# Attention scores of a two-layer encoder: the products with the low parts of K as pairs of 64-row tiles

## The chip, the cores and the metric

The kernel runs on one core of a Trainium2 chip. The metric is the time of one execution on the device in microseconds (us), the median of three runs. The engines named below are PE (TensorE, which multiplies; PEld are its weight loads), DVE (VectorE), ACT (ScalarE), POOL (GpSimd) and SP (SyncE, which issues most DMAs). A change of 0.2% is about the least that a measurement of this kernel can tell from none.

## What is computed

The reference is a stack of two layers over 256 tokens of 1024 channels. Each layer has one combined input projection, three mixers (a short convolution, a pooling mixer, attention), a gated sum through W_o, and a SwiGLU feed-forward block. What the change touches is the scores of the attention:

```
scores = einsum("bnqhgd,bnkhd->bhgnqk", qb, kb) * HEAD_DIM ** -0.5     # 16 heads, 4 KV heads, HEAD_DIM 64
scores = where(valid, scores + bias, NEG_INF)                         # |key - query| <= 128, T5 bias
m = maximum(max(scores), sink);  p = exp(scores - m)
p = p / (sum(p) + exp(sink - m));  out = einsum(p, v)
```

With 256 tokens and a window of 128 on both sides, each block of 128 queries sees all 256 keys, and the mask rides in the bias.

## The kernel before

All matrix work is done in split precision: an fp32 operand is held as a high part (rounded, type fp32r) and a low part (what is left), and a product is the sum of three products, high by high, high by low and low by high (`mm3`, lines 160 to 164). Weights come as blocks of 128 x 128 in the order in which they are used; `convert` (lines 128 to 137) splits 8 blocks at a time into `hi` (ACT) and `lo` (DVE). The program is 7877 products on PE, and almost all are of one kind: load a 128 x 128 block, stream 256 columns against it.

Attention is done for two heads at a time, in 8 groups `t` per layer, 16 in the program. `qs[t]` holds two tiles of 128 rows, one per head `j` of the group: for head 0 the 64 rows 0 to 63 are the high parts of Q and rows 64 to 127 the low parts; for head 1 it is the other way round. For each KV head, `kk[v][0]` holds the high parts of K twice, in both halves of the rows, so that one product of 128 rows gives high Q by high K plus low Q by high K. `kk[v][1]` holds the low parts of K in the 64 rows that carry the high parts of Q, and zeros in the other 64 (set once, line 206). One product of 128 rows with it gives high Q by low K; half of its rows multiply by zero.

`att_scores` (lines 340 to 365) makes for each of two blocks `b` of 128 queries and each head `j` those two products, 8 in all, into a PSUM bank per block `b`: the halves of the bank are the two heads. DVE then reads each half, adds the bias and takes the row maximum in one instruction (line 353); ACT takes the exponentials (line 358), and DVE multiplies by the reciprocal of the sum (line 363). `att_transpose` transposes the probabilities on PE (line 374), `att_pv` multiplies by V (line 389).

These steps are sprinkled into the long projection: `tick()` is called after each output tile of the projection (24 products of PE), and the table `steps` says that the scores of group `t` go at tick 4 + int(4.3 t), its transposes 4 ticks later and its products with V 6 ticks later (constants SC0, SCD, TRD, PVD on line 768). Where the transposes of one group and the scores of the next fall on one tick, the scores go first. PSUM has two pools of four banks: `newB` for the projections, `newA` for the scores, transposes and V products of attention, used in rotation.

Of the kernel before, what the change touches and what calls it, by code (L numbers as in the profile page):

```python
# [16 lines left out]
P = 128  # L17
D = 1024
T = 256
# [4 lines left out]
EPS = 1e-6  # L24
NEG = -1e30
# [8 lines left out]


def plan_layer(last):
    """Order in which the 128 x 128 weight blocks (matrix, k, n) of a layer are used."""
    out = []

    def inner(mat, ns, nk=KT):  # L40
        for n in ns:
            for k in range(nk):
                out.append((mat, k, n))

    def outer(mat, ns, nk=KT):
        for k in range(nk):
            for n in ns:
                out.append((mat, k, n))

    outer("in", (CK, CK + 1, CV, CV + 1))  # L50
    for q in range(2):
        inner("in", [CQ + 4 * q + j for j in range(4)])
    inner("in", [CGA + n for n in range(8)])
    for n in range(8):
        inner("in", (CC + n, CX + n, CB + n))
    inner("in", (CU, CU + 1))
    inner("a", range(8))
    for n in range(8):
        inner("in", (CGP + n, CGT + n))
        if n % 2 == 1 and n < 7:  # L60
            inner("in", (CU + n + 1, CU + n + 2))
        inner("t", (n,))
        out.extend(("pool", k, n) for k in range(2))
        if n >= 2:
            out.extend(("o", n - 2, m) for m in range(8))
    for j in range(4):
        out.extend(("o", k, m) for k in (6, 7) for m in (2 * j, 2 * j + 1))
    for q in range(NQ):
        ns = (2 * q, 2 * q + 1, FT + 2 * q, FT + 2 * q + 1)
        if q == 0:  # L70
            outer("gu", ns)
        else:
            inner("gu", ns)
        if q >= 1:
            for k in (2 * q - 2, 2 * q - 1):
                out.extend(("down", k, m) for m in range(8))
    ks = (2 * NQ - 2, 2 * NQ - 1)
    if last:
        for k in ks:
            out.extend(("down", k, m) for m in range(8))  # L80
    else:
        for j in range(4):
            out.extend(("down", k, m) for k in ks for m in (2 * j, 2 * j + 1))
    return out
# [6 lines left out]
def trunk(ctx, tc, wst, xT, chp, sinkb, rb, invc, gfin, ident_d, out):  # L91
    nc = tc.nc
    V, S, G, PE = nc.vector, nc.scalar, nc.gpsimd, nc.tensor
# [12 lines left out]
        uid[0] += 1  # L106
        return f"{s}{uid[0]}"

# [1 line left out]
    plan = []  # L110
    for l in range(L):
        plan += [(l,) + key for key in plan_layer(l == L - 1)]
# [55 lines left out]
    def half(j):  # L168
        return slice(j * T, (j + 1) * T)

# [1 line left out]
    warm = const.tile([P, T], F32R, name="warm")  # L172
    V.memset(warm.bitcast(F32), 0.0)
    epst = const.tile([P, 1], F32, name="epst")
# [6 lines left out]
    x = act.tile([P, KT, T], F32, name="x")  # L181
# [9 lines left out]
    V.memset(ones, 1.0)  # L191
    ident = const.tile([P, P], F32, name="ident")
    G.dma_start(ident, ident_d)
    # [0 | I | 0]
    ident2 = const.tile([P, 3 * P], F32R, name="ident2")
    G.memset(ident2.bitcast(F32), 0.0)
    G.tensor_copy(ident2[:, P:2 * P], ident)
# [2 lines left out]
    inv = const.tile([P, 4, 2, 8], F32, name="inv")  # L200
    G.dma_start(inv, invc)

    # kk[kv]: (high parts of K in both halves of the rows, low parts in one half and zeros in the other)
    kk = [[act.tile([P, T], F32R, name=f"kk{v}{i}") for i in range(2)] for v in range(4)]
    for v in range(4):
        V.memset(kk[v][1].bitcast(F32), 0.0)
    ups = [act.tile([P, T + 16], F32, name=f"up{i}") for i in range(2)]
    for u in ups:
        V.memset(u, 0.0)
    # vt[key tile]: per pair of KV heads (a, b) the columns [a high | a low | b low | b high]  # L210
    vt = [act.tile([P, 2, 4, 64], F32R, name=f"vt{kt}") for kt in range(2)]

    stab = dpool.tile([16, 512], F32, name="stab")

    def build_bias():
        """stab[h, i] = rel_bias[bucket(255 - i), h] inside the window, NEG outside."""
        st = tmp.tile([16, 512], F32, name="st", tag="t2", bufs=8)
        G.memset(st, NEG)
        G.tensor_copy(st[:, 248:255], rbt[:, 17:24][:, ::-1])
        G.tensor_copy(st[:, 255:263], rbt[:, 0:8])  # L220
        for i, (a, b) in enumerate(RANGES):
            G.tensor_copy(st[:, 255 - b:256 - a], rbt[:, 24 + i:25 + i].to_broadcast([16, b - a + 1]))
            G.tensor_copy(st[:, 255 + a:256 + b], rbt[:, 8 + i:9 + i].to_broadcast([16, b - a + 1]))
        G.dma_start(stab, st)
# [12 lines left out]
        t = pool.tile([P, 2, T], F32R, name=nm(name), tag=tag, bufs=bufs)  # L237
        return t[:, 0, :], t[:, 1, :]

# [1 line left out]
    def xg_tiles(l, gi, j, st):  # L241
        """x tiles 2j, 2j+1 times the gain, split."""
        for k in (2 * j, 2 * j + 1):
            g = ch[:, l, gi, k:k + 1]
            h, lo = pair(act, "xz", 8, "xg")
            if j < XJ:
                V.tensor_scalar(h, x[:, k], g, None, op0=ALU.mult)  # L247
            else:
                S.activation(h, x[:, k], AF.Copy, scale=g)
            V.scalar_tensor_tensor(lo, x[:, k], g, h.bitcast(F32), op0=ALU.mult, op1=ALU.subtract)  # L250
            st["xg"].append((h, lo))

    def squares(j, st):
        """Squares of x tiles 2j, 2j+1, added up."""
        sq = tmp.tile([P, 2, T], F32, name=nm("sq"), tag="t2", bufs=8)
        S.activation(sq, x[:, 2 * j:2 * j + 2], AF.Square)
        if j == 0:
            st["acc"] = sq
        else:
            G.tensor_tensor(st["acc"], st["acc"], sq, op=ALU.add)  # L260
        if j == 3:
            s1 = tmp.tile([P, T], F32, name=nm("s1"), tag="t1", bufs=10)
            st["add"] = G.tensor_tensor(s1, st["acc"][:, 0], st["acc"][:, 1], op=ALU.add)
            st["sum"] = s1

    def preload(func, src):
        """Has the activation table of func loaded once src is there."""
        d = tmp.tile([P, 1], F32, name=nm("pre"), tag="pre", bufs=2)
        S.activation(d, src, func)

    def rsqrt(r, sd, ms):
        """r = ms ** -0.5 from the table's square root, one Newton step on top."""
        V.reciprocal(r, sd)
        V.tensor_tensor(ms, ms, r, op=ALU.mult)
        V.tensor_tensor(ms, ms, r, op=ALU.mult)
        V.tensor_scalar(ms, ms, -0.5, 1.5, op0=ALU.mult, op1=ALU.add)
        V.tensor_tensor(r, r, ms, op=ALU.mult)
# [13 lines left out]
        st["q"], st["ps"] = rr, ps  # L291

    def norm_rows(st):
        """The tokens' factors as rows, the same on all partitions."""
        rr, ps = st["q"], st["ps"]
        for i in range(4):
            tb = i % 2
            PE.matmul(ps[:, T:], rr[:, i:i + 1].to_broadcast([P, P]), ident2[:, P - tb * P:3 * P - tb * P],
                      start=(i == 0), stop=(i == 3))
        r = tmp.tile([P, T], F32, name=nm("r"), tag="rbc", bufs=2)  # L300
        S.activation(r, ps[:, T:], AF.Copy)
        st["r"] = r
# [21 lines left out]
    def newA(name="a"):  # L324
        return psA.tile([P, 2 * T], F32, name=nm(name), tag="A")
# [10 lines left out]
        for k in range(nk):  # L336
            mm3(dst, (l, mat, k, n), xs[koff + k][0], xs[koff + k][1], start=(k == 0), stop=(k == nk - 1))

# [1 line left out]
    def att_scores(l, t, qs, st):  # L340
        bias = st["bias"].pop(t)
        ss = []
        for b in range(2):
            ps = newA("sc")
            cs = slice(b * P, (b + 1) * P)
            for j in range(2):
                kh, kl = kk[2 * (t // 4) + j]
                PE.matmul(ps[:, half(j)], qs[t][j][:, cs], kh, start=True, stop=False)  # L348
                PE.matmul(ps[:, half(j)], qs[t][j][:, cs], kl, start=False, stop=True)
            s = tmp.tile([P, 2, T], F32, name=nm("s"), tag="t2", bufs=8)  # L350
            sm = tmp.tile([P, 10], F32, name=nm("sm"), tag="sm", bufs=6)
            for j in range(2):
                V.tensor_tensor_reduce(s[:, j], ps[:, half(j)], bias[:, j, b * P:b * P + T], 1.0,
                                       sk[:, l, 2 * t + j:2 * t + j + 1], ALU.add, ALU.max, sm[:, j:j + 1])
            V.tensor_scalar(sm[:, 2:4], sm[:, 0:2], -1.0, None, op0=ALU.mult)  # L355
            V.tensor_tensor(sm[:, 4:6], sk[:, l, 2 * t:2 * t + 2], sm[:, 2:4], op=ALU.add)
# [39 lines left out]
        split(h, lo, f)  # L396
        st["ao"][t] = (h, lo)

# [1 line left out]
    def t1(name):  # L400
        return tmp.tile([P, T], F32, name=nm(name), tag="t1", bufs=10)

    def mixer(l, st):
        xg = st["xg"]
        def kv_out():
            norm_rows(st)
            r = st["r"]
            # K reversed in the tokens
            for p in range(2):
                kf = t1("kf")  # L410
                V.tensor_tensor(kf[:, ::-1], kb[:, half(p)], r, op=ALU.mult)
                for j in range(2):
                    rr = slice(64 * j, 64 * j + 64)
                    other = slice(64 - 64 * j, 128 - 64 * j)
                    kh, kl = kk[2 * p + j]
# [13 lines left out]
        qs = []  # L429
# [73 lines left out]
        def pool_mixer(n, bank, j):  # L503
# [7 lines left out]
            for d in (1, 2, 4)[:g]:  # L511
# [1 line left out]
                lo_, hi_ = lo_ + d, hi_ - d  # L513
                V.tensor_tensor(s2[:, lo_:hi_], s[:, lo_ - d:hi_ - d], s[:, lo_ + d:hi_ + d], op=ALU.add)
                s = s2
            # the ends divide by their own counts: the constant is window / count there
            e = bass.AP(tensor=s.tensor, offset=s.offset + 8, ap=[list(s.ap[0]), [T - 8, 2], [1, 8]])
            V.tensor_tensor(e, e, inv[:, g], op=ALU.mult)
            pf = t1("pf")
# [181 lines left out]
    for l in range(L):  # L701
# [13 lines left out]
        else:  # L715
            fms = [tmp.tile([P, 8], F32, name=nm("fm"), tag="sm", bufs=6) for _ in range(2)]

            def sums(tb):
                """fm[0], fm[1]: sums of squares of the halves; fm[2]: the first as a share of the mean, + EPS."""
                fm = fms[tb]  # L720
                for hh in range(2):
                    y = xn[2 * tb + hh]
# [40 lines left out]
MH = 1  # L763
XJ = 1
POOLW = (2, 4, 8, 16)
# distances in the window that share one of the T5 buckets 8..15 (exact buckets below 8)
RANGES = ((8, 11), (12, 15), (16, 22), (23, 31), (32, 45), (46, 63), (64, 90), (91, 128))
SC0, SCD, TRD, PVD = 4, 4.3, 4, 6

# [63 lines left out]
```

## Time and profile before

| | |
|---|---|
| three runs, us | 981.97, 981.01, 981.03 |
| median, us | 981.03 |
| span of the profiled execution, first to last instruction, us | 980.1 |
| PE busy in it, us (share) | 968.1 (99%) |
| PE weight loads busy, us (share) | 954.4 (97%) |
| DVE busy, us (share) | 715.7 (73%) |
| ACT busy, us (share) | 554.0 (57%) |
| mean granted clock of TensorE, of full speed | 0.998 |

The profile is of one execution; the 0.9 us between its span and the median are what lies outside the first and the last instruction, and how executions differ. Busy times of PE are sums of pieces in which at least one product was running; products overlap, so a single one lasts 0.28 us while the next starts 0.12 us after it.

### The profile page before, as it was taken

How to read it: one execution, taken by the hardware profiler on the slowest of the kernel's cores; microseconds unless marked ns; L12 is line 12 of the kernel's file. 1: busy time of each engine (PE TensorE's matmuls, PEld its weight loads, DVE VectorE, ACT ScalarE, POOL GpSimd, SP SyncE). 2: the span in 40 equal slices, each digit the busy share in tenths (PEclk: the TensorE clock that was granted, in tenths of full speed). 3: DMA queues.
4: the chain of work that ended last, by engine and by line, in shares of the span. 5: the costliest groups of instructions: out<-in, count | busy, mean ns of one | idle time of the engine just before them, and what ended most of it. 6: DMA issues, size and time to landing. Idle time of an engine off the chain costs nothing.

```text
span 980.1 us, 19200 instructions
## 1 busy us (share of the span) xinstructions
PE 968.1 (99%) x7877; PEld 954.4 (97%) x7877; DVE 715.7 (73%) x1332; ACT 554.0 (57%) x931; POOL 45.7 (5%) x66
## 2 busy tenths in 40 slices
PE   8999999999999999999999999999999999999996
PEld 7999999999999999999999999999999999999995
DVE  7899898567668955545589898985777697555554
ACT  5866776654456544444477576765554564444443
POOL 5100000000001000000020000000000020000001
PEclk9999999999999999999999999999999999999999
DMA  8755544555554455455443745445554555545531
GB/s 279 254 193 197 189 161 163 197 180 183 189 199 171 174 189 199 173 178 205 178 172 130 248 163 188 161 143 174 192 193 173 172 194 189 200 170 204 184 129 43
DMA packets 27112, 178.12 MB, mean 182 GB/s; under 512 B 3280, under 2 KB 3808, under 8 KB 6800
## 3 DMA queue, kind: packets, MB, share of 16 engines
q1 hardware_dynamic: 24912, 169.93, 49.1%
q0 software_dynamic: 2112, 6.97, 2.5%
q8 instruction: 61, 1.00, 0.4%
q14 instruction: 27, 0.22, 0.1%
HBM read 175.80 MB, written 1.08 MB: 180 GB/s over the span
## 4 chain that ended last, share of the span: by engine, by line
PE 97%; DMA 1%; DVE 1%; SPq 0%; ACT 0%; issue 0%; DVEq 0%; ACTq 0%
PE b L162 25%; PE b L164 25%; PE b L163 25%; PE dn L164 2%; PE dn L162 2%; PE dn L163 2%; PE dn L617 2%; PE dn L616 2%; PE dn L615 2%; PE wo L162 2%; PE wo L163 2%; PE o L389 2%; PE wo L164 2%; PE pt L374 1%; DMA x<-xT 1%; PE sc L348 1%
## 5 line engine op out<-in xcount | busy, mean ns | idle before, releaser
L136 DVE TENSOR_TENSOR lo<-raw,hi 128x1024 fp32r<-128x1024 f32 (+1 forms) x321 | 390.0, 1222 | 215.2 <-ACT hi L135 214.4
L135 ACT ACTIVATE hi<-raw 128x1024 fp32r<-128x1024 f32 (+1 forms) x321 | 337.2, 1055 | 333.1 <-PE b L163 215.0
L162 PE MATMUL b<-h,hi 128*128 128x256 f32 x1344 | 379.8, 283 | 0.0
L164 PE MATMUL b<-h,lo 128*128 128x256 f32 x1344 | 378.4, 282 | 0.0
L163 PE MATMUL b<-h,hi 128*128 128x256 f32 x1344 | 378.3, 281 | 0.0
L162 PEld LDWEIGHTS b<-h,hi 128*128 128x128 f32 x1344 | 253.2, 188 | 0.2
L163 PEld LDWEIGHTS b<-h,hi 128*128 128x128 f32 x1344 | 253.1, 188 | 0.2
L164 PEld LDWEIGHTS b<-h,lo 128*128 128x128 f32 x1344 | 253.1, 188 | 0.0
L163 PE MATMUL b<-xg,hi 128*128 128x256 f32 x448 | 126.6, 283 | 1.6 <-DVE xg L250 1.6
L162 PE MATMUL b<-xg,hi 128*128 128x256 f32 x448 | 126.3, 283 | 1.1 <-DVE xg L247 0.8
L164 PE MATMUL b<-xg,lo 128*128 128x256 f32 x448 | 126.0, 282 | 0.0
L163 PEld LDWEIGHTS b<-xg,hi 128*128 128x128 f32 x448 | 84.4, 188 | 2.3 <-DVE xg L250 2.2
L162 PEld LDWEIGHTS b<-xg,hi 128*128 128x128 f32 x448 | 84.2, 188 | 1.6 <-issue 1.1
L164 PEld LDWEIGHTS b<-xg,lo 128*128 128x128 f32 x448 | 84.4, 188 | 0.0
L164 PE MATMUL dn<-fa,lo 128*128 128x256 f32 x176 | 49.5, 281 | 0.0
L163 PE MATMUL dn<-fa,hi 128*128 128x256 f32 x176 | 49.5, 281 | 0.0
L162 PE MATMUL dn<-fa,hi 128*128 128x256 f32 x176 | 49.5, 281 | 0.0
L260 POOL TENSOR_TENSOR sq<-sq,sq 128x512 f32<-128x512 f32 x12 | 16.2, 1353 | 507.3 <-DVE xg L250 315.5
L358 ACT ACTIVATE s<-s,sm 128x256 f32<-128x256 f32 x64 | 31.8, 500 | 13.0 <-DVE sm L355 13.0
L162 PE MATMUL b<-z,hi 128*128 128x256 f32 x128 | 36.4, 284 | 0.0
L164 PE MATMUL b<-z,lo 128*128 128x256 f32 x128 | 36.1, 282 | 0.0
L164 PE MATMUL b<-ao,lo 128*128 128x256 f32 x128 | 36.0, 282 | 0.0
(174 smaller groups left out, 1537.9 us busy)
## 6 DMA issues: line engine op xcount, KB each, us to landing
raw<-wst SPq DMA_DIRECT2D x158, 1024.0 KB, 4.9
bias<-stab POOLq DMA_DIRECT2D x16, 384.0 KB, 3.9
raw<-wst SPq DMA_DIRECT2D x3, 512.0 KB, 7.7
out<-xn SPq DMA_DIRECT2D x4, 256.0 KB, 2.0
x<-xT SPq DMA_DIRECT2D x3, 256.0 KB, 8.2
raw<-wst SPq DMA_DIRECT2D x2, 256.0 KB, 4.2
gf<-gfin POOLq DMA_DIRECT2D x2, 256.0 KB, 3.8
x<-xT SPq DMA_DIRECT2D x2, 128.0 KB, 4.6
```

What stands on the lines that cost most here:

```text
L135: S.activation(hi[:, s], raw[:, s], AF.Copy)
L136: V.tensor_tensor(lo[:, s], raw[:, s], hi[:, s].bitcast(F32), op=ALU.subtract)
L162: PE.matmul(dst, wh, xh, start=start, stop=False, skip_group_check=skip)
L163: PE.matmul(dst, wh, xl, start=False, stop=False, skip_group_check=skip)
L164: last_mm[0] = PE.matmul(dst, wl, xh, start=False, stop=stop, skip_group_check=skip)
L260: G.tensor_tensor(st["acc"], st["acc"], sq, op=ALU.add)
L348: PE.matmul(ps[:, half(j)], qs[t][j][:, cs], kh, start=True, stop=False)
L358: S.activation(s[:, j], s[:, j], AF.Exp, bias=sm[:, 2 + j:3 + j], accum_out=sm[:, 6 + j:7 + j])
L389: PE.matmul(ps[:, half(j)], vv, pts[kt][i][:, half(j)], start=(kt == i == 0), stop=(kt == i == 1))
L615: PE.matmul(d, ah[:, cs], wh, start=(k == 0), stop=False)
L616: PE.matmul(d, ah[:, cs], wl, start=False, stop=False)
L617: PE.matmul(d, al[:, cs], wh, start=False, stop=(k == FT - 1))
```

## The change

Only `att_scores` is changed; everything else in the diff are comments that go, and shifted line numbers. The two PSUM banks of a group are now one per head (`banks[j]`), with the two blocks of queries as halves. All four products with the high parts of K come first, as before with 128 rows. Then come the four products with the low parts, each with only those 64 rows that hold something other than zeros: rows 0 to 63 for head 0, rows 64 to 127 for head 1, in turn. A product of 64 rows uses a tile of 64 x 128 of the array; the two heads use the upper and the lower tile. The number of products, the columns that each streams and the sums are the same.

```diff
     def att_scores(l, t, qs, st):
         bias = st["bias"].pop(t)
         ss = []
+
+        banks = [newA("sc") for _ in range(2)]
         for b in range(2):
-            ps = newA("sc")
-            cs = slice(b * P, (b + 1) * P)
             for j in range(2):
-                kh, kl = kk[2 * (t // 4) + j]
-                PE.matmul(ps[:, half(j)], qs[t][j][:, cs], kh, start=True, stop=False)
-                PE.matmul(ps[:, half(j)], qs[t][j][:, cs], kl, start=False, stop=True)
+                PE.matmul(banks[j][:, half(b)], qs[t][j][:, b * P:(b + 1) * P], kk[2 * (t // 4) + j][0],
+                          start=(b == 0), stop=False, skip_group_check=True)
+
+        for b in range(2):
+            for j in range(2):
+                r = slice(64 * j, 64 * j + 64)
+                PE.matmul(banks[j][:, half(b)], qs[t][j][r, b * P:(b + 1) * P], kk[2 * (t // 4) + j][1][r],
+                          start=False, stop=True, skip_group_check=True)
+        for b in range(2):
             s = tmp.tile([P, 2, T], F32, name=nm("s"), tag="t2", bufs=8)
             sm = tmp.tile([P, 10], F32, name=nm("sm"), tag="sm", bufs=6)
             for j in range(2):
-                V.tensor_tensor_reduce(s[:, j], ps[:, half(j)], bias[:, j, b * P:b * P + T], 1.0,
+                V.tensor_tensor_reduce(s[:, j], banks[j][:, half(b)], bias[:, j, b * P:b * P + T], 1.0,
                                        sk[:, l, 2 * t + j:2 * t + j + 1], ALU.add, ALU.max, sm[:, j:j + 1])
```

On PE, the scores of the first group in the program, between two output tiles of the projection (b66). In the rows sc67 and sc70 are the banks of the two blocks of queries; kk00 and kk10 are the high parts of K for the two heads, kk01 and kk11 the low parts. Before:

```order
L164 MATMUL b66_850<-xg8_191,lo16_720 128x256
L348 MATMUL sc67_879<-kk00_133,q31_510 128x256
L349 MATMUL sc67_879<-kk01_134,q31_510 128x256
L348 MATMUL sc67_879<-kk10_135,q31_510 128x256
L349 MATMUL sc67_879<-kk11_136,q31_510 128x256
L348 MATMUL sc70_897<-kk00_133,q31_510 128x256
L349 MATMUL sc70_897<-kk01_134,q31_510 128x256
L348 MATMUL sc70_897<-kk10_135,q31_510 128x256
L349 MATMUL sc70_897<-kk11_136,q31_510 128x256
L162 MATMUL b66_850<-xg1_158,hi17_790 128x256
```

The same place of the changed kernel, where sc67 and sc68 are the banks of the two heads and lines 347 and 353 are the products with the high and the low parts:

```order
L164 MATMUL b66_850<-xg8_191,lo16_720 128x256
L347 MATMUL sc67_879<-kk00_133,q31_510 128x256
L347 MATMUL sc68_880<-kk10_135,q31_510 128x256
L347 MATMUL sc67_879<-kk00_133,q31_510 128x256
L347 MATMUL sc68_880<-kk10_135,q31_510 128x256
L353 MATMUL sc67_879<-kk01_134,q31_510 128x256
L353 MATMUL sc68_880<-kk11_136,q31_510 128x256
L353 MATMUL sc67_879<-kk01_134,q31_510 128x256
L353 MATMUL sc68_880<-kk11_136,q31_510 128x256
L162 MATMUL b66_850<-xg1_158,hi17_790 128x256
```

High and low products no longer alternate: each group has one passage from 128-row products to 64-row tiles and one back, and within the four the tile, the bank and the head alternate.

On DVE, the readers of those banks (ISA stands for the fused add and maximum, and for the read of its accumulator into sm), before:

```order
L353 ISA s68_884,sm69_885<-sc67_879,bias16_342,sk_129 128x256
L353 ISA sm69_885 128x1
L353 ISA s68_884,sm69_885<-sc67_879,bias16_342,sk_129 128x256
L353 ISA sm69_885 128x1
L353 ISA s71_902,sm72_903<-sc70_897,bias16_342,sk_129 128x256
```

and in the changed kernel:

```order
L359 ISA s69_889,sm70_890<-sc67_879,bias16_342,sk_129 128x256
L359 ISA sm70_890 128x1
L359 ISA s69_889,sm70_890<-sc68_880,bias16_342,sk_129 128x256
L359 ISA sm70_890 128x1
L359 ISA s71_902,sm72_903<-sc67_879,bias16_342,sk_129 128x256
```

The readers are the same in number, size and place; they now go from bank to bank, so that both banks are held until the last of the four reads, where the first was free after two.

## Rows read from the trace of the kernel before

**Rows 1.** The profile's page: the span, the busy time of each engine with its share and its count of instructions, and the clock granted to TensorE in 40 slices of the span (9 is 90% or more).

```profile
span 980.1 us, 19200 instructions
...
PE 968.1 (99%) x7877; PEld 954.4 (97%) x7877; DVE 715.7 (73%) x1332; ACT 554.0 (57%) x931; POOL 45.7 (5%) x66
...
PEclk9999999999999999999999999999999999999999
```

**Rows 2.** Everything that PE waited for in the whole span: line, releaser, then us in total, times, longest.

```profile
PE b L163 <- DVE xg L250: 1.6, 2, 0.9
PE wps L180 <- DVE epst L175: 1.2, 1, 1.2
PE b L162 <- DVE xg L247: 0.8, 1, 0.8
PE b L162 <- ACT xg L249: 0.3, 1, 0.3
```

**Rows 3.** Busy time of each engine in the two stretches that hold the attention of the two layers: start and end, length, busy us and count of PE, PEld, DVE, ACT and POOL, granted clock, DMA share, GB/s.

```profile
59.00:186.00 127.00, 127.00 (x1077) 127.00 (x1076) 111.78 (x291) 85.01 (x188) 5.69 (x8) 1.00 0.56 191
...
540.00:670.00 130.00, 130.00 (x1103) 130.00 (x1102) 111.01 (x291) 87.59 (x192) 3.61 (x5) 1.00 0.53 182
```

**Rows 4.** All instructions that write or read the scores' banks: line, engine, count, shortest, median and longest duration in ns, first and last start.

```profile
L348 PEld LDWEIGHTS sc<-kk,q x64: 187/188/190, 59.9 to 645.0; 128*128 128x128 f32 x64
L348 PE MATMUL sc<-kk,q x64: 274/281/287, 60.0 to 645.1; 128*128 128x256 f32 x64
...
L349 PE MATMUL sc<-kk,q x64: 279/281/285, 60.1 to 645.2; 128*128 128x256 f32 x64
```

**Rows 5.** The timeline of PE and PEld around the first group's scores: start, duration, line, operation.

```profile
59.99 0.28 PE L348 MATMUL sc<-kk,q 128*128 128x256 f32 x1
59.99 0.19 PEld L349 LDWEIGHTS sc<-kk,q 128*128 128x128 f32 x1
60.11 0.28 PE L349 MATMUL sc<-kk,q 128*128 128x256 f32 x1
...
60.94 0.28 PE L162 MATMUL b<-xg,hi 128*128 128x256 f32 x1
```

**Rows 6.** The same timeline where the transposes of the first group follow the scores of the second (columns as above; x8 is eight instructions merged).

```profile
73.17 0.28 PE L349 MATMUL sc<-kk,q 128*128 128x256 f32 x1
73.18 0.90 PEld L374 LDWEIGHTS pt<-ident,s 128*128 128x128 f32 x8
73.28 1.04 PE L374 MATMUL pt<-ident,s 128*128 128x128 f32 x8
...
74.05 0.19 PEld L162 LDWEIGHTS b<-h,hi 128*128 128x128 f32 x1
...
74.28 0.27 PE L163 MATMUL b<-h,hi 128*128 128x256 f32 x1
```

**Rows 7.** PE and PEld at 18.75 us, where PE starts again after a wait, with nothing loaded ahead.

```profile
18.75 0.39 PE L163 MATMUL b<-xg,hi 128*128 128x256 f32 x1 [0.87 <-DVE xg L250]
18.97 0.28 PE L164 MATMUL b<-xg,lo 128*128 128x256 f32 x1
...
18.75 0.19 PEld L163 LDWEIGHTS b<-xg,hi 128*128 128x128 f32 x1 [1.08 <-DVE xg L250]
18.86 0.19 PEld L164 LDWEIGHTS b<-xg,lo 128*128 128x128 f32 x1
```

**Rows 8.** DVE's reads of the first group's and the second group's scores and the end of the first group's probabilities, from the timeline of DVE.

```profile
63.98 0.48 DVE L353 CUSTOM_DVE_ANT_0 s<-sc,bias,sk 128x256 f32<-128x256 f32 x1
...
69.80 0.62 DVE L363 TENSOR_SCALAR s<-s,sm 128x256 f32<-128x256 f32 x2
...
74.01 0.48 DVE L353 CUSTOM_DVE_ANT_0 s<-sc,bias,sk 128x256 f32<-128x256 f32 x1
...
74.48 0.47 DVE L353 CUSTOM_DVE_ANT_0 s<-sc,bias,sk 128x256 f32<-128x256 f32 x1
```

**Rows 9.** The chain that ended last, in order of time: start, us, what. The first product of the first group with V, and the end of the program.

```profile
80.02 0.95 PE o L389 x8
...
971.76 0.24 PE dn L617
972.02 0.70 DVE xn L723
```

## The prediction

> **What bounds the kernel now.** I read the page first, then what PE waits for, then the stretches of the attention, then single instructions. The page shows PE and its weight loads busy for 99% and 97% of a span of 980.1 us, at a granted clock of 9 in every slice, against 73% for DVE [rows 1]. The list of PE's waits has four lines, 3.9 us together [rows 2]; none is at an instruction of the attention. In both stretches that hold the attention PE is busy for the whole of it, 127 of 127 us and 130 of 130 [rows 3]. The chain that ended last leaves PE only at 971.76 us, for the work after the last product [rows 9]. So the order on PE is the schedule: what a group of scores costs is the distance between the product before and the one after, and the time of the kernel moves by 16 times the change of that distance as long as nobody else becomes late.
>
> The timeline gives the distance. The eight products of a group begin at 59.99 and the projection goes on at 60.94 [rows 5]: 0.95 us, or 0.119 us per product, though each lasts 0.28 us [rows 4]. That pace rests on overlap: the load for the next product (0.19 us) starts in the moment in which the present product starts [rows 5], so a load is never seen.
>
> **The change part by part.** The products with the high parts are the same four per group and are only put next to each other: 4 x 0.119 us before and after, no gain, no loss. The two counts of 64 [rows 4] are 128 products for 16 groups, 8 each.
>
> The four products with the low parts keep their columns, 256 each, but take half of the rows. If the tiles of the two heads work side by side, four slots become two: 2 x 0.119 = 0.24 us less per group, 3.8 us for 16. If they go one after the other, nothing is saved, or next to nothing: products that stream only 128 columns follow each other at 0.109 us (eight loads from 73.18 to 74.05) [rows 6], which is all that four loads in a row would gain, 4 x 0.01 us per group, 0.6 us in all. I take 3.8 us, since the tiles share neither rows nor bank. [...]
>
> Against that stand the two passages per group, from 128 rows to tiles and back, 32 in the program. The trace has no passage of this sort, so its price is bounded from both sides. From below: nothing, if loads go on being made ahead. The nearest thing in the trace is the passage from products to transposes and back, and it costs nothing: transposes start at 73.28, 0.11 us after the last score at 73.17, and nine instructions later, at 74.28, the pace is as before [rows 6]. It could not be below nothing, since no instruction goes. In between: one load that is not made ahead. Where PE begins with nothing loaded, the first product lasts 0.39 us instead of 0.28 and the next load starts 0.11 us after the first [rows 7], so that a load that must be waited for costs 0.11 us. From above: a full stop, in which the next load starts only when the product in flight has ended. Then the next product begins 0.28 + 0.11 us after the last one instead of 0.12: 0.27 us per passage. If only the products stop and the load is made under the running one, it is 0.28 - 0.12 = 0.16 us.
>
> So the sum per program is 32 passages less 3.8 us: at nothing, -3.8 us; at 0.11, 3.5 - 3.8 = -0.3 us; at 0.16, 5.1 - 3.8 = +1.3 us; at 0.27, 8.6 - 3.8 = +4.8 us. I take a stop: the array is asked for another layout than the one the running product uses, and the load of the new layout goes to the very cells that product runs through, which is more than transposes change (those use the same 128 rows and columns). For the load I have no row that decides, and take the middle of 0.16 and 0.27, 0.215 us: 6.9 - 3.8 = +3.1 us. [...]
>
> What hides the rest: DVE has the same instructions. The reads of the first group begin at 63.98, almost 3 us after the last product has ended, and its probabilities are done by 70.42 (69.80 + 0.62), while the transposes that need them start at 73.18 [rows 6, 8]. A shift of the scores by 0.3 us is covered there; if it were not, PE would stand for what is missing at 8 groups per layer. The banks: before, the first bank was free after the second read, now only after the third, one read later (0.48 us) [rows 8]. The next but one user of the pool, the product with V, starts at 80.02 [rows 9], and the second group's last read ends at 74.95 (74.48 + 0.47) [rows 8], 5 us earlier, so this costs nothing. No DMA, no queue of SP or POOL and no weight load of the stream is moved. Whatever PE gains or loses goes on to the end, since PE is the chain up to 971.76 us [rows 9] and nothing before it limits how early the weights are there: PE's only waits are four [rows 2].
>
> The sum is made against the profiled execution, 980.1 us: 980.1 + 3.1 = 983.2 us. The median of the runs, 981.03, is 0.9 us above that span; I let this stand and predict 981.03 + 3.1 = 984.1 us.
>
> **The rivals.** First, the passage is free and the tiles run side by side. For it: products and transposes pass into each other at no cost [rows 6], and PE loads ahead everywhere [rows 5]. Against it: both of those keep the layout of the array. Price: 16 x 0.24 us, so 981.03 - 3.8 = 977.2 us, faster. It decides as soon as a passage costs less than about 0.06 us: 32 x 0.06 is 1.9 us, which leaves 1.9 us of gain, the 2.0 us (0.2%) that a measurement of this kernel can tell from no change.
>
> Second, a passage costs one load that was not made ahead, 0.11 us, and no more [rows 7]: -0.3 us, 980.7 us, no difference. For it: this is the only price that the trace shows for an interrupted row of loads. Against it: it supposes that products of both layouts may be in the array together.
>
> Third, the change does not do what it says: the two tiles, or their loads, go one after another, at 0.109 us each [rows 6], and the passages cost what I forecast. Then 6.9 - 0.6 = +6.3 us, 987.3 us. For it: on PE loads are the tightest thing, at 97% busy [rows 1], and 0.109 is barely under 0.119; a row of loads is not shortened by fewer rows. Against it: the two tiles lie in different rows of the array and banks.
>
> **How the numbers follow.** I give the forecast (a stop at each passage, tiles side by side; +1.3 to +4.8 us, 982.3 to 985.9) a chance of 0.43, the free passage 0.25, the load alone 0.20, and the tiles one after another 0.12. The free passage is all of "faster", 0.25. "Within 0.2%" (2.0 us) has the load alone and the lower end of the forecast, where the passage costs 0.16 to 0.18 us, 0.09 of its 0.43: 0.29. "Slower" has the rest of the forecast and the third rival, 0.34 + 0.12 = 0.46. The range must hold the free passage, which has more than two in ten, so it begins at 976.9, just under 977.2; at the upper end it goes to 987.0, beyond the dearest passage (985.9) and short of the middle of the third rival, most of which is left out, about one in ten.
>
> **What would show it.** In the changed kernel's timeline the distance from the last product with the high parts to the first after the group, which is 5 x 0.119 = 0.59 us where nothing changes: 0.36 us if the passage is free, 0.58 with the load alone, 0.68 to 0.90 by my forecast, about 1.0 in the third rival. Each step has its own sign: the two products of a pair that start within some hundredths of a us show that tiles run side by side; the first 64-row load that starts only at the end of the product before it (0.28 us after that one's start) shows the stop, one that starts with the product shows loading ahead. The forecast falls if the first tile's load starts with the last high product and the first product with it 0.12 us later; the whole reasoning falls if PE waits for DVE at a transpose, or if the time moves by something else than 16 times that distance.

## The result and the profile after

The changed kernel takes 983.64 us, median of 10 runs, against 981.65 us for the kernel before, also of 10: 2.0 us more, a ratio of 1.0022 with a 95% interval of 1.0013 to 1.0030. It is slower, by just about what can be told from no change. Of the kernel with a shorter product (below), one execution of five was slow, with 2251 us, and is not in its median.

The page of the changed kernel, the lines that answer to [rows 1], and what PE waits for, which answers to [rows 2]:

```profile
span 982.4 us, 19192 instructions
...
PE 970.6 (99%) x7877; PEld 953.1 (97%) x7877; DVE 715.4 (73%) x1332; ACT 554.3 (56%) x931; POOL 45.9 (5%) x66
...
PEclk9999999999999999999999999999999999999999
```

```profile
PE wps L180 <- DVE epst L175: 1.2, 1, 1.2
PE b L162 <- ACT xg L249: 1.0, 1, 1.0
PE b L162 <- DVE xg L247: 0.8, 1, 0.8
PE b L163 <- DVE xg L250: 0.8, 1, 0.8
```

The span is 2.3 us longer. The waits of PE are 3.8 us, against 3.9, all at the start; DVE and ACT do what they did; the clock is the same in every slice. So the time is neither a wait for another engine nor the clock; it lies in the order on PE itself. The instructions on the scores' banks (line, engine, count, shortest, median and longest duration in ns), which answer to [rows 4]:

```profile
L347 PE MATMUL sc<-kk,q x64: 274/279/283, 60.3 to 646.9; 128*128 128x256 f32 x64
L353 PEld LDWEIGHTS sc<-kk,q x64: 182/184/186, 60.9 to 647.2; 64*128 64x128 f32 x64
L353 PE MATMUL sc<-kk,q x64: 275/330/387, 60.9 to 647.4; 64*128 64x256 f32 x64
```

The low products are 64-row tiles as announced, and half of them last up to 0.39 us. A duration of 0.39 instead of 0.28 was, in the kernel before, the mark of a product whose load was not made ahead [rows 7]. The timeline of the first group, which answers to [rows 5]; x4 is four instructions merged, and the later lines are from narrower stretches of the same timeline, where they come apart into pairs:

```profile
60.33 0.63 PE L347 MATMUL sc<-kk,q 128*128 128x256 f32 x4
60.88 0.51 PE L353 MATMUL sc<-kk,q 64*128 64x256 f32 x4
61.32 0.39 PE L162 MATMUL b<-xg,hi 128*128 128x256 f32 x1
61.54 0.29 PE L163 MATMUL b<-xg,hi 128*128 128x256 f32 x1
...
61.43 0.19 PEld L163 LDWEIGHTS b<-xg,hi 128*128 128x128 f32 x1
...
60.56 0.19 PEld L347 LDWEIGHTS sc<-kk,q 128*128 128x128 f32 x1
...
60.67 0.28 PE L347 MATMUL sc<-kk,q 128*128 128x256 f32 x1
60.88 0.19 PEld L353 LDWEIGHTS sc<-kk,q 64*128 64x128 f32 x2
...
60.99 0.19 PEld L353 LDWEIGHTS sc<-kk,q 64*128 64x128 f32 x2
...
61.11 0.28 PE L353 MATMUL sc<-kk,q 64*128 64x256 f32 x2
```

This is the whole mechanism. The last high product starts at 60.67, and no load starts with it: the last load before it starts at 60.56. The loads of the first pair start at 60.88, 0.21 us later, both at once (x2); the next two loads at 60.99, 0.11 us after the first two; the second pair runs at 61.11, both products at once. Then the same again: the next load of 128 rows waits until 61.32, 0.21 us after 61.11. Its product is recorded from 61.32 too, but lasts 0.39 us, 0.11 more than one that was loaded ahead, and the load behind it starts at 61.43; I take 61.43 for its real start, as elsewhere the next load starts together with the product [rows 5]. The tiles do work side by side, four products in two slots, and each passage costs 0.21 + 0.11 - 0.12 = 0.20 us. From the first high product to the first product after the group it is 61.43 - 60.33 = 1.10 us, against 0.95 [rows 5].

Where the transposes of another group follow, the way back is cheaper. The changed kernel at the place of [rows 6]:

```profile
72.82 0.40 PE L347 MATMUL sc<-kk,q 128*128 128x256 f32 x2
...
73.38 0.51 PE L353 MATMUL sc<-kk,q 64*128 64x256 f32 x4
73.81 1.09 PE L380 MATMUL pt<-ident,s 128*128 128x128 f32 x8
...
74.86 0.27 PE L163 MATMUL b<-h,hi 128*128 128x256 f32 x1
```

In the kernel before, the same eight scores begin at 72.34, and the product at 74.28 [rows 6] is 1.94 us later:

```profile
72.34 0.28 PE L348 MATMUL sc<-kk,q 128*128 128x256 f32 x1
```

Now it is 74.86 - 72.82 = 2.04 us, 0.10 more instead of 0.15: the eight transposes last 1.09 us for 1.04 [rows 6], so only 0.05 us of the transposes' first load is seen. By the table of steps, 10 of the 16 groups are followed by transposes (ticks 4, 8, 12, 21 and 25 after the first, in each layer) and 6 by the projection: 10 x 0.10 + 6 x 0.15 = 1.9 us. The runs say 2.0. All 16 groups keep to the two values, read finer 0.106 and 0.154 us, with which the sum is 2.0 as well.

### The profile page after: what moved, and what is told of

Read it like the earlier page. It is cut to its first block, busy times and chain, and to the rows that moved or that the text cites. A ratio compares the mean times of both kernels' runs of the same rounds, so it can differ in the third digit from the quotient of the medians.

```text
span 982.4 us, 19192 instructions
## 1 busy us (share of the span) xinstructions
PE 970.6 (99%) x7877; PEld 953.1 (97%) x7877; DVE 715.4 (73%) x1332; ACT 554.3 (56%) x931; POOL 45.9 (5%) x66
## 4 chain that ended last, share of the span: by engine, by line
PE 98%; DMA 1%; SPq 0%; DVE 0%; ACT 0%; issue 0%; DVEq 0%; ACTq 0%
PE b L162 25%; PE b L163 25%; PE b L164 25%; PE dn L163 2%; PE dn L162 2%; PE dn L164 2%; PE dn L623 2%; PE dn L621 2%; PE dn L622 2%; PE wo L162 2%; PE pt L380 2%; PE wo L163 2%; PE o L395 2%; PE wo L164 2%; PE sc L347 1%; DMA raw<-wst 1%
```

## The experiments

The theory (S in the expectations): the array stops at each passage between 128-row products and 64-row tiles, 0.20 us each, and pairs of tiles run side by side, which saves 0.24 us per group. The rivals: the banks, the order or the readers make the loss (B); a passage is only a load not made ahead (L); the tiles run one after another (O). Two letters come in later: W is named where it is tested, and where two groups are put together, L stands for another rival, a price that belongs to the tiles and not to the passages.

**Everything but the tiles.**

```diff
-                r = slice(64 * j, 64 * j + 64)
+                r = slice(0, P)
```

> Everything of the change but the tiles: one bank per head, high products first, readers from bank to bank, and the low products with all 128 rows again (half of them zeros). Theory S (the array stops at each passage between 128 rows and tiles, 0.20 us each, and the tiles of a pair run side by side): no passage and no pair, so 8 slots of 0.119 us per group as before, 981.65 us, within 0.2%. Rival B (the loss comes from the banks, the order or the readers, and the tiles are worth nothing or something): the loss stays or grows, 983.6 us, or up to 987 if the pairs did save 3.8 us.

Measured: 981.92 us against 981.6, ratio 1.0002 (0.9993 to 1.0011). The group in its timeline:

```profile
59.65 0.63 PE L347 MATMUL sc<-kk,q 128*128 128x256 f32 x4
60.11 0.64 PE L353 MATMUL sc<-kk,q 128*128 128x256 f32 x4
60.59 0.28 PE L162 MATMUL b<-xg,hi 128*128 128x256 f32 x1
```

60.59 - 59.65 = 0.94 us, eight slots, as before. Banks per head, the order of the products and the readers cost nothing that the times can tell (the interval reaches from -0.7 to +1.1 us), and the group takes the same eight slots; rival B falls, and the 2.0 us are the tiles'.

**Four passages per group.** The block's low pair directly behind its high products:

```diff
         for b in range(2):
             for j in range(2):
                 PE.matmul(banks[j][:, half(b)], qs[t][j][:, b * P:(b + 1) * P], kk[2 * (t // 4) + j][0],
                           start=(b == 0), stop=False, skip_group_check=True)
-
-        for b in range(2):
             for j in range(2):
                 r = slice(64 * j, 64 * j + 64)
```

> The same products with the same tiles, but the two pairs are each put behind the high products of their block of queries: four passages per group in place of two. Theory S: 32 more passages at 0.20 us, +6.4 us on the changed kernel's 983.6, 990.0 us. Rival L (a passage is a load that isn't made ahead, 0.11 us, and the rest of the loss lies elsewhere): +3.5 us, 987.1. Rival B: passages cost nothing, 983.6.

Measured: 989.79 us against 981.6, ratio 1.0083 (1.0069 to 1.0097). The timeline shows the stop four times:

```profile
59.60 0.40 PE L348 MATMUL sc<-kk,q 128*128 128x256 f32 x2
59.92 0.39 PE L352 MATMUL sc<-kk,q 64*128 64x256 f32 x2
60.24 0.50 PE L348 MATMUL sc<-kk,q 128*128 128x256 f32 x2
60.67 0.38 PE L352 MATMUL sc<-kk,q 64*128 64x256 f32 x2
60.98 0.39 PE L162 MATMUL b<-xg,hi 128*128 128x256 f32 x1
```

Every first product behind a passage lasts 0.38 us or more (in the lines of two, their common stretch), and the 32 passages more cost 989.79 - 983.64 = 6.2 us, 0.19 each. Theory S gave 990.0, rival L 987.1.

**Tiles without pairs.** Head 1's low products have 128 rows and come first, then head 0's two tiles:

```diff
-        for b in range(2):
-            for j in range(2):
-                r = slice(64 * j, 64 * j + 64)
+        for j in (1, 0):
+            for b in range(2):
+                r = slice(0, P) if j else slice(0, 64)
```

> Only head 0's low products are 64-row tiles, head 1's have 128 rows, and stand before them: two passages per group, but no pair. Theory S: nothing is saved, 32 passages at 0.20 us, +6.4 us on the kernel before, 988.0 us. Rival O (the tiles of a pair run one after another and the saving comes from something else): as the changed kernel, 983.6 us. Rival B: 983.6 as well or less.

Measured: 987.62 us against 981.6, ratio 1.0059 (1.0045 to 1.0072): 6.0 us for 32 passages, 0.19 us each, with nothing saved. Rival O falls. So the pairs of the changed kernel save the difference, 987.62 - 983.64 = 4.0 us, where 3.8 was worked out. The passage is now measured without a pair. The pair is not measured without a passage: its 4.0 us are a difference between two kernels, so that 6.0 - 4.0 gives the loss is no test of its own. What shows its size apart from that is the timeline, two slots for four products, and the kernel with two groups at one place below.

**Another order of the tiles.** Upper, upper, lower, lower:

```diff
-        for b in range(2):
-            for j in range(2):
+        for j in range(2):
+            for b in range(2):
                 r = slice(64 * j, 64 * j + 64)
```

> The tiles in the order upper, upper, lower, lower in place of upper, lower in turn. Products start in the order in which they stand, so the second and the third can start together and the others not: three slots in place of two, +0.12 us per group, +1.9 us on the changed kernel, 985.5 us. If only products that stand next to each other from the start of the row pair up and none does here: four slots, +3.8, 987.4 us. If PE finds pairs for itself whatever the order: 983.6 us.

Measured: 983.58 us against 981.6, ratio 1.0021 (1.0012 to 1.0029), the time of the changed kernel. What I expected, three slots, was wrong. Its loads and its second pair of products in narrow stretches, and for comparison below them the kernel of the tiles without pairs, in which two tiles of the same rows follow each other:

```profile
60.83 0.19 PEld L353 LDWEIGHTS sc<-kk,q 64*128 64x128 f32 x2
...
60.94 0.19 PEld L353 LDWEIGHTS sc<-kk,q 64*128 64x128 f32 x2
...
61.06 0.28 PE L353 MATMUL sc<-kk,q 64*128 64x256 f32 x2
```

```profile
60.95 0.18 PEld L353 LDWEIGHTS sc<-kk,q 64*128 64x128 f32 x1
...
60.95 0.29 PEld L353 LDWEIGHTS sc<-kk,q 64*128 64x128 f32 x2
```

Two loads for the same rows take 0.29 us together, 0.18 and 0.11 more; here two loads start together and last 0.19. The records do not name the tile, and that two loads which start together are not both for the upper tile is argued from that comparison. But each record in the kept trace says whether its product counts up the semaphore (a counter) that DVE waits for before it reads the scores (10 waits, 8.7 us in this trace). In the program the last product into each bank does, here the second and the fourth tile; in the trace it is the two that start last, at 61.06, in all 16 groups. So the first lower tile, third in the program, went with the first upper one, and overtook the second.

**Two groups at one place.** Eight high products, then eight tiles, in four banks; every 9 ticks, with the transposes of the two groups 5 and 6 ticks after and the V products 7 and 8 (the steps of one tick also go in the order of the list, a line that is not shown):

```diff
+    def att_products(l, ts, qs):
+        bks = {t: [newA("sc") for _ in range(2)] for t in ts}
+        for t in ts:
+            for b in range(2):
+                for j in range(2):
+                    PE.matmul(bks[t][j][:, half(b)], qs[t][j][:, b * P:(b + 1) * P], kk[2 * (t // 4) + j][0],
+                              start=(b == 0), stop=False, skip_group_check=True)
+        for t in ts:
...
     def att_scores(l, t, qs, st):
+        if t % 2 == 0:
+            st["bk"] = att_products(l, (t, t + 1), qs)
...
+            at0 = 4 + 9 * (t // 2)
+            for at, f in ((at0, att_scores), (at0 + 5 + t % 2, att_transpose), (at0 + 7 + t % 2, att_pv)):
```

> Two groups of scores at one place: eight products with the high parts, then eight tiles, in all four banks of the pool; every second passage goes. Transposes and V products of the two groups follow one tick apart. Theory S: 16 passages in place of 32, 16 x 0.20 - 3.8 = -0.6 us against the kernel before, 981.0 us, 2.6 us under the changed kernel. Rival L (the price belongs to the tiles, not to the passages: each 64-row pair is slow by itself): as the changed kernel, 983.6 us. Rival W (the saving is there but four banks at once make PE wait for DVE and ACT): PE has waits at transposes or V products, and the time is above 982.5 us.

Measured: 982.22 us against 981.66, ratio 1.0005 (0.9996 to 1.0014). 1.4 us of the loss are gone, not 2.6. The timeline of the first two groups, and the waits of PE:

```profile
61.28 0.74 PE L351 MATMUL sc<-kk,q 64*128 64x256 f32 x8
61.95 0.38 PE L162 MATMUL b<-xg,hi 128*128 128x256 f32 x1
```

```profile
PE b L163 <- DVE xg L250: 1.6, 2, 0.9
PE wps L180 <- DVE epst L175: 1.2, 1, 1.2
PE b L162 <- DVE xg L247: 0.8, 1, 0.8
PE b L162 <- ACT xg L249: 0.6, 1, 0.6
PE b L163 <- DVE z L234: 0.5, 2, 0.2
```

Eight tiles, up to the load of the way back, take 61.95 - 61.28 = 0.67 us where four take 61.32 - 60.88 = 0.44: two more pairs for 0.23 us, a slot of 0.12 us for each pair. So the price belongs to the passage, and rival L falls. But the last line of the waits is new: two groups of softmax at once make DVE late with `z` of the convolution, 0.5 us of idle PE in two waits by the list. That is rival W in another form than expected: the waits are in the projection and not at transposes or V products, and the time is under the 982.5 us that W asked for. They explain 0.5 of the 1.2 us that are missing; the rest is within the interval of this measurement, about 0.9 us either way, and stays open.

**Two groups, earlier.** The same every 8 ticks, transposes 4 and 5 ticks after, V products 6 and 7 (the lines are against the kernel above):

```diff
-            at0 = 4 + 9 * (t // 2)
-            for at, f in ((at0, att_scores), (at0 + 5 + t % 2, att_transpose), (at0 + 7 + t % 2, att_pv)):
+            at0 = 4 + 8 * (t // 2)
+            for at, f in ((at0, att_scores), (at0 + 4 + t % 2, att_transpose), (at0 + 6 + t % 2, att_pv)):
```

> Two groups of scores at one place as before, but every 8 ticks in place of 9, with transposes 4 and V products 6 ticks after, so that the attention ends before the products that PE waited for. Theory S: the group's saving of 0.063 us per pair of heads' groups pair stays, 8 x 0.063 = 0.5 us, and with no new waits the time is 981.2 us, 0.05% under the kernel before, too little to be told from it. Rival W: PE waits again, at transposes that now come earlier, and the time is 982.2 us or more.

Measured: 981.30 us against 981.49, ratio 0.9997 (0.9988 to 1.0006), and the list has no wait of PE but those at the start. The timeline has a small one: the eight high products of the second visit, and beside them those of the first, and DVE's last read of an earlier product with V (in brackets DVE's own idle time before it and what ended that):

```profile
59.85 1.11 PE L345 MATMUL sc<-kk,q 128*128 128x256 f32 x8
...
88.13 1.25 PE L345 MATMUL sc<-kk,q 128*128 128x256 f32 x8
...
88.21 0.42 DVE L407 TENSOR_TENSOR of<-oo,o 64x256 f32<-64x256 f32 x1 [0.44 <-ACT oo L406]
```

By the rotation of the pool the last of the four banks is the one that DVE still reads until 88.63, and PE loses 0.14 us there, once in each layer. So four banks at one place are not quite free. The kernel is 2.3 us under the changed kernel and can't be told from the kernel before: 3.8 us of pairs pay for 16 passages at 0.20 us, 3.2 us together, and nearly nothing is left over.

**A shorter product before the passage.** The last high product, and the last pair of tiles, each cut into two of 128 columns:

```diff
+                for c in ((0, T),) if b * j == 0 else ((0, P), (P, T)):
+                    PE.matmul(banks[j][:, b * T + c[0]:b * T + c[1]], qs[t][j][:, b * P:(b + 1) * P],
+                              kk[2 * (t // 4) + j][0][:, c[0]:c[1]],
...
+            for c in ((0, T),) if b == 0 else ((0, P), (P, T)):
...
```

> The last product before each passage is cut into two of 128 columns: the last high product, and the last pair of tiles. If the stop lasts until the last column of the product in flight has gone through, the next load starts 0.05 us sooner after the start of that product, 0.16 us in place of 0.21, at both passages. If the stop is a fixed time from the start of the product, it stays 0.21. Time: each cut adds a slot of 0.11 us less 0.01, twice per group, +3.2 us on the changed kernel with a fixed stop, 986.8 us, and 1.6 us less, 985.2 us, where the stop ends with the columns.

Measured: 985.24 us, the median of four executions, against 981.66, ratio 1.0035 (1.0021 to 1.0048). That is 1.6 us over the changed kernel, where a stop that ends with the columns gave 1.6 and a fixed one 3.2. The timeline at the first passage:

```profile
59.35 0.19 PEld L348 LDWEIGHTS sc<-kk,q 128*128 128x128 f32 x1
...
59.41 0.27 PE L348 MATMUL sc<-kk,q 128*128 128x128 f32 x1
59.61 0.19 PEld L356 LDWEIGHTS sc<-kk,q 64*128 64x128 f32 x2
```

The load starts 0.20 us after the recorded start of the short product, as if the stop were fixed; but that start is recorded before the product's own load was through (it lasts 0.27 us with half the columns, where a product of 256 lasts 0.28). Its load starts at 59.35, so by the 0.11 us that a product needs after a load that it waits for (0.39 for 0.28 us, [rows 7]), it began at 59.46, and the next load came 0.15 us later, not 0.21: 0.06 us sooner, for which the expectation had 0.05 as an estimate. Counted from the recorded end, which the profile models and does not observe, it is the same everywhere: 59.41 + 0.27 = 59.68, and the load starts 0.07 before it; in the changed kernel 60.67 + 0.28 = 60.95, and the load starts at 60.88, 0.07 before it. Time and timeline agree: here the stop waited for the product in flight, not for a fixed time.

**Transposes before the scores**, where both fall on one tick:

```diff
-            for f, t in reversed(steps.pop(clock[0], [])):
+            for f, t in steps.pop(clock[0], []):
```

> As the changed kernel, but where transposes and scores fall on one tick the transposes go first, so that every group of tiles is followed by a product of the projection and none by a transpose. If the way out of the tiles is cheaper in front of a transpose, because its load is seen for 0.05 us and not 0.11, then all 16 groups cost 0.155 us more than before in place of 6, and the time is 984.1 us, 0.5 us over the changed kernel. If it is the place in the program that makes those 10 groups cheaper, they stay at 0.106 and the time at 983.6 us.

Measured: 983.96 us against 981.49, ratio 1.0025 (1.0016 to 1.0034). That is 2.5 us over the kernel before, the 16 x 0.155 that was expected, but between 983.96 and 983.64 the times alone decide nothing. The trace does. The way back of the second group, now into the projection:

```profile
73.19 0.51 PE L353 MATMUL sc<-kk,q 64*128 64x256 f32 x4
73.63 0.39 PE L162 MATMUL b<-h,hi 128*128 128x256 f32 x1
73.85 0.29 PE L163 MATMUL b<-h,hi 128*128 128x256 f32 x1
```

From the first tile to the second product of the projection it is 73.85 - 73.19 = 0.66 us, as at the first group of the changed kernel (61.54 - 60.88), and the first product shows its whole load, 0.39 for 0.28 us. At the same place of the program the changed kernel had the cheap way back, so it is the load of a transpose that is short, not the place.

## Why the prediction was right

It gave 984.1 us, in a range of 976.9 to 987.0, and slower as the likeliest; 983.64 was measured. That the two are so near is half luck. The change was forecast at +3.1 us and is +2.0; the 981.03 us to which it was added, a median of three, is 0.6 us under the median of ten. The sign that was announced came out: from the last high product to the first after the group it is 61.43 - 60.67 = 0.76 us, inside the 0.68 to 0.90 of the forecast and clear of the rivals' 0.36, 0.58 and 1.0.

- *PE's order is the schedule, 16 times the change of one distance.* Right: no wait came or went, and 10 x 0.10 + 6 x 0.15 us is the difference of the medians within 0.1 us. That the distance would not be the same in all groups was not foreseen: in front of a transpose the way back costs 0.05 us less.
- *Two slots saved per group, 3.8 us.* Right. The trace before has no product of fewer than 128 rows [rows 4 to 6], so that the tiles run side by side was an assumption; the changed kernel has two slots in the timeline, with both loads of the first pair at 60.88, and between tiles without pairs and tiles with them lie 4.0 us. The third rival, tiles one after another, is out.
- *A stop at each passage, between 0.16 and 0.27 us, taken at 0.215.* The mechanism was right, and both of its parts: no load is made ahead, and the load waits for the product, 0.21 us after its start. Its size is 0.20 us: 0.21 + 0.11 - 0.12. The upper bound had the load wait for the recorded end, 0.28 us after the start; it starts 0.07 us sooner. With that in the upper bound, and the load seen in full, the sum is 32 x 0.20 - 3.8 = 2.6 us, and the cheaper way back in 10 groups takes 0.5 us off. The middle of the two bounds came out near by luck as much as by reason: the load is not half hidden, the stop is shorter. Of the reason given for a stop, the runs bear out the change of layout: the load waits 0.21 us where 128-row products and 64-row tiles follow each other. That it goes to cells in use is not enough by itself: in the kernel without pairs two tiles of the same rows follow each other with their loads 0.11 us apart.
- *The first rival, a free passage*, leaned on the transposes, which pass into products and back at no cost [rows 6]. They do, 0.11 us after the last score, and that says nothing of a passage to fewer rows. At both passages it is 0.21 us until the next load, 0.07 us short of the recorded end of the product ahead of it, and between the first upper and the first lower tile there is no gap: both loads start at 60.88.
- *DVE and the banks cost nothing.* Right within the interval: the kernel with everything but the tiles is at 1.0002. The first bank is held until the third of the four reads, as the prediction has it, not until the last, as the section on the change says.

## What to carry to other kernels

Here two tiles side by side saved a slot of 0.12 us for each pair, but the way into the tiles and out again cost two stops of 0.20 us, 0.4 us per visit. By my estimate from these figures a visit must hold at least four pairs before it earns anything, and the changed kernel's has two. With four the time could not be told from the kernel before; more than four was not run. Count visits, not products, before tiling rows: gather the small products of several steps at one place if banks and readers allow; here that took 1.4 and 2.3 us off the changed kernel. And when a change is an exchange of two terms, run one of them without the other: here everything without the tiles showed that the loss is theirs, and tiles without pairs showed what the passages cost alone.

## What was not expected of the hardware

- The order of tiles in the program did not matter for the pairs: upper, upper, lower, lower takes 983.58 us as upper, lower in turn takes 983.64. I had counted on products starting in program order, as the scores of the kernel before do [rows 5]. The trace shows another order: the two products that count up DVE's semaphore, second and fourth in the program, are both recorded from 0.22 us after the other two, in all 16 groups.
- A stop ended 0.07 us before the recorded (modelled) end of the product that it waited for, with 256 columns (60.88 against 60.95) and with 128 (59.61 against 59.68).
- The load of a transpose that was not made ahead is seen for 0.05 us (eight transposes last 1.09 us for 1.04), that of a product for 0.11 (0.39 us for 0.28).
